# Feed-forward blocks on four PSUM banks each, the sums of their seven-product groups formed in place, and sevens in two of three feature groups of a stage's last two down blocks

## Chip, cores and metric

One core of a Trainium2 chip runs the whole program in one launch. The metric is the device time of one execution in microseconds (us); a time that is named for the kernel is the median of its runs.

## The reference

Two layers of a hybrid block on 256 rows of width 2048, all in float32: a mixer (gated delta rule and a linear recurrence in layer 0, two attentions in layer 1) and behind each mixer a feed-forward part of inner width 5632. Only the feed-forward parts and the norms beside them matter here:

```python
def swiglu(hn, w_gate, w_up, w_down):
    return (jax.nn.silu(hn @ w_gate) * (hn @ w_up)) @ w_down
...
    for layer in range(DEPTH):
...
            h = h + gdn_rglru_mixer(rmsnorm(h, ab_norm[j]), ab_w_in[j], ab_conv_qkv[j], ab_a_log[j],
...
            h = h + fox_moba_mixer(rmsnorm(h, cd_norm[j]), cd_w_in[j], cd_f_bias[j], cd_w_out[j])
        h = h + swiglu(rmsnorm(h, ffn_norm[layer]), ffn_w_gate[layer], ffn_w_up[layer], ffn_w_down[layer])
    return rmsnorm(h, final_norm)
```

## The kernel before, in words

**Split operands.** Every weight tile is loaded as float32 (128x1024: 256 rows of the contraction by 512 columns, 0.5 MB), rounded by ScalarE to `hi` (`whi` or `thi`, L547), and VectorE subtracts to get `lo` (`wlo` or `tlo`, L560). The activations are kept as such a pair too: `X` (the mixer's output, normed), `hid` (silu(gate)*up, turned). A product takes three TensorE passes, x_hi·w_hi, x_hi·w_lo and x_lo·w_hi (L419 to L421), all 128 rows by 512 columns.

**Plain steps and sevens.** A feed-forward block makes a 256x1024 result (two row halves t, two column halves i, so four PSUM banks `F[t,i]`). It is a *gate/up* block (512 gate and 512 up columns, contraction 2048 from `X`, four feature groups of 512) or a *down* block (1024 columns of the output, contraction over the `hid` of the stage, three or four feature groups). A *plain* step takes one weight tile and serves both row halves: 12 matmuls. A feature group done plainly is four such steps, 48 matmuls. A group done *by sevens* is seven steps of one product each, six matmuls a step, 42 in all: it multiplies sums of the activation quarters (`comb`, made ahead by `combine`) by sums of the weight tiles b11, b12, b22 and b21.

**Where the sevens accumulate.** Four of the seven products are needed in more than one of the four results. They go to banks `M0` to `M3` of their own (pool `msp`, four banks, tag `ms`), and the other three to `F` (pool `acc`, four banks). At the block's end `ends` copies M0 out and adds M2, M3 and M1 into a 128x4x512 tile `e` in SBUF (L431 to L434); `values` then adds each `F` to `e`, applies the scales and silu and multiplies (L721, L722, L727); `residual` adds `h` to `e` and then `F` (L741, L746). The banks of one block are freed by these reads, and the next block takes the same `acc` and `ms` banks.

**Weight sums.** In a seven VectorE forms T = b11+b12 (L485), T += b22 and T += b21 (L492); b12+b22 is made by one accumulating DMA from GpSimd's queue (L487). `load` (L166) gives each tile a buffer of `wr` (three) or `raw4` (four); it runs inside `ahead`, four steps ahead of the step's matmuls, and the first 12 loads of a phase take `wr` alone (`loads[0] = -12` in `phase`, L74).

**Order.** `ffn` (L657) runs 11 gate/up blocks and 6 down blocks as three stages of 4, 4 and 3 gate/up blocks with two down blocks behind each. `groups` and `down` say how many feature groups go by sevens: none in the first block, two of four in the others, two in the down blocks of the first two stages and one of three in those of the last. `steps` mixes plain steps and sevens, three plain steps in front and three behind. From the second block on VectorE, ScalarE and TensorE run in the order written (`stream`, `manual_schedule`); before that the scheduler places the instructions. SyncE (SP) issues all loads in one queue, and a load that waits for its buffer holds those behind it.

**Around it.** The mixer's last projection ends with `norm_then`: for each 512 columns `sumsq` squares `h` into a scratch tile `junk` (L316 to L319), and `to_x` transposes `h` into `X` (L328 to L330). A mixer phase and a feed-forward phase use the same SBUF space for their pools, so a tile of the feed-forward phase outside `wr` can be written only when the last reader or writer of what lay there is done.

Of the kernel before, what the change touches and what calls it, by code (L numbers as in the profile page):

```python
# [47 lines left out]
def body(tc, A, out):  # L48
# [266 lines left out]
    def sumsq(g, *ts):  # L315
        for t in ts or range(2):  # L316
            j = (mx.tile([128, 1024], F32, name="junk", tag="T", bufs=2)[:, 0:512] if more else
                 mx.tile([128, 512], F32, name="junk", tag="t2", bufs=4))
            S.activation(j, h[:, t, g * 512:(g + 1) * 512], AF.Square, accum_out=ssp[:, t, g:g + 1])  # L319
# [69 lines left out]
    def combine(f, r=None):  # L389

        c = mx.tile([128, 4, 2, 128], F32, name="cc4", tag="T", bufs=2)
# [12 lines left out]
    def combine_x(x4, r=None):  # L404

        f = mx.tile([128, 4, T], F32, name="cf", tag="T", bufs=2)
# [31 lines left out]
    class Step:  # L438


        def __init__(self, high, use, unit=None):
            self.high, self.use, self.unit = high, use, unit

    def steps(src, x, comb, nd, early, late):

        ns = len(comb)
        plain = [(i, u) for m in range(nd) if m not in comb for u in (2 * m, 2 * m + 1) for i in range(2)]
        n, F, M = len(plain) // 2, {}, {}

        def bank(t, i):  # L450
            if (t, i) not in F:
                F[t, i] = Bank(acc.tile([128, 512], F32, name=f"F{t}{i}", tag="acc"), n + (ns if t * i == 0 else 0))
            return F[t, i]

        def bank7(j):
            if j not in M:
                M[j] = Bank(ms([128, 512], f"M{j}"), ns)
            return M[j]

        def xs(k, t):  # L460
            return [x(k)[:, j, t * 128:(t + 1) * 128] for j in range(2)]

        def high(i, u, b, name):
            def f():
                b[name] = load(src(i, u))
                return b[name]
            return f

        def simple(i, u):
            b = {}  # L470

            def use(w, tt=(0, 1)):
                for t in tt:
                    bank(t, i).add(lambda kk: xs(2 * u + kk, t), w)
            return Step(high(i, u, b, "b"), use, (i, use))

        def seven(m):
            b = {}
            cx = lambda i: lambda kk: [comb[m]()[:, j, i, kk] for j in range(2)]
            q = lambda j, t: lambda kk: xs(4 * m + 2 * j + kk, t)  # L480

            def first():
                load_b12()
                b["t"] = mx.tile([128, 1024], F32, name="T", tag="T", bufs=2)
# [1079 lines left out]
```

## Time and profile before

| | |
|---|---|
| median of 3 runs | 2218.5 us (2218.19 to 2218.76) |
| span of the profiled execution, first to last instruction | 2217.3 us, 1.2 under the median of the runs; its own time is not listed apart |
| TensorE, VectorE, ScalarE busy | 99%, 88%, 60% |
| feed-forward part of layer 0, first to last matmul | 430.3 to about 1098 us |
| feed-forward part of layer 1 | 1517.5 to 2208.2 us |
| loads there, 0.5 MB each | 264 a part from SP, 30 accumulating ones a part from GpSimd |

A busy time is a union of what the profile records; a matmul's record is longer than the distance to the next one, so TensorE's rate is read from the starts of its instructions and not from its busy share. A row of the timeline gives start, length, engine, line and form; in brackets stands the engine's idle time before it and what ended it.

### The profile page before, as it was taken

To read this page: it belongs to the slowest core of one execution; us is meant where nothing else is said; L and a number is where in the kernel's file an instruction comes from. 1 tells how busy PE (TensorE), PEld (TensorE's weight loads), DVE (VectorE), ACT (ScalarE), POOL (GpSimd) and SP (SyncE) were. 2 spreads that over 40 slices of the span, in tenths; PEclk is the share of its full clock that TensorE was granted. 3 is DMA by queue.
4 is the path that set the end of the run, shared out by engine and by line. 5 is a ranking of instruction groups with operands and counts; after the bars stand their busy time and mean duration, and the time that the engine had idled before them with its cause. 6 is when DMAs were issued, how large, how long until landed. Compare 5 with 4: busy or idle time off the path is not lost.

```text
span 2217.3 us, 30619 instructions
## 1 busy us (share of the span) xinstructions
PE 2200.4 (99%) x10960; PEld 1840.2 (83%) x10960; DVE 1961.3 (88%) x2664; ACT 1333.7 (60%) x1787; POOL 54.0 (2%) x66
## 2 busy tenths in 40 slices
PE   9999999999999999999999999999999999999998
PEld 8888888888888888888888888888888888888886
DVE  8899676679999999999996688857899999999998
ACT  6786664556655666466664554545666566655665
POOL 0000000000000000000000000000000000000000
PEclk9999999999999999999999999999999999999999
DMA  7545446667777778677664565556678777777784
GB/s 284 158 145 167 136 151 188 204 210 222 235 226 247 211 215 246 214 229 235 195 201 154 154 188 171 162 181 218 204 214 237 232 224 222 237 224 233 232 243 138
DMA packets 126569, 453.79 MB, mean 205 GB/s; under 512 B 14128, under 2 KB 15664, under 8 KB 126288
## 3 DMA queue, kind: packets, MB, share of 16 engines
q1 hardware_dynamic: 117488, 420.10, 58.2%
q0 software_dynamic: 8640, 31.46, 8.5%
q8 instruction: 86, 1.41, 0.3%
q14 instruction: 67, 0.55, 0.1%
q10 hardware_dynamic: 288, 0.27, 0.0%
HBM read 449.68 MB, written 2.10 MB: 204 GB/s over the span
## 4 chain that ended last, share of the span: by engine, by line
PE 88%; DVE 8%; issue 2%; DMA 1%; ACT 1%; DVEq 0%; ACTq 0%; POOLq 0%; SPq 0%
PE F L420 14%; PE F L419 14%; PE F L421 14%; PE Pw L201 11%; PE Pw L206 6%; PE M L421 5%; PE M L419 5%; PE M L420 5%; PE Px L305 3%; PE Px L307 3%; PE Px L306 3%; DVE wlo L560 1%; PE Ph L673 1%; DVE e L721 1%; DVE tlo L560 1%
## 5 line engine op out<-in xcount | busy, mean ns | idle before, releaser
L181 ACT CAST whi<-raw 128x1024 fp32r<-128x1024 f32 x245 | 256.8, 1051 | 261.7 <-PE Pw L201 85.3
L547 ACT CAST whi<-raw 128x1024 fp32r<-128x1024 f32 x362 | 372.0, 1048 | 51.1 <-PE F L421 31.1
L182 DVE TENSOR_TENSOR wlo<-raw,whi 128x1024 fp32r<-128x1024 f32 x245 | 299.0, 1222 | 114.7 <-PE Pw L206 37.2
L201 PE MATMUL Pw<-X,whi 128*128 128x512 f32 x1088 | 388.3, 400 | 0.0
L206 PE MATMUL Pw<-X,wlo 128*128 128x256 f32 x1088 | 304.6, 280 | 0.2
L419 PE MATMUL F<-whi,X 128*128 128x512 f32 x698 | 273.1, 391 | 0.6 <-DVE h L746 0.6
L421 PE MATMUL F<-whi,X 128*128 128x512 f32 x698 | 272.1, 390 | 0.0
L560 DVE TENSOR_TENSOR wlo<-raw,whi 128x1024 fp32r<-128x1024 f32 x214 | 260.6, 1220 | 9.2 <-ACT whi L547 5.3
L420 PE MATMUL F<-wlo,X 128*128 128x512 f32 x650 | 253.2, 390 | 0.0
L201 PEld LDWEIGHTS Pw<-X,whi 128*128 128x128 f32 x1088 | 204.2, 188 | 47.2 <-issue 0.5
L547 ACT CAST whi<-T 128x1024 fp32r<-128x1024 f32 x110 | 116.1, 1055 | 197.2 <-DVE T L492 119.1
L206 PEld LDWEIGHTS Pw<-X,wlo 128*128 128x128 f32 x1088 | 205.3, 189 | 1.6 <-DVE wlo L182 0.7
L560 DVE TENSOR_TENSOR tlo<-raw,whi 128x1024 fp32r<-128x1024 f32 x148 | 180.6, 1220 | 7.9 <-ACT whi L547 6.0
L547 ACT CAST thi<-raw 128x1024 fp32r<-128x1024 f32 x166 | 173.5, 1047 | 13.6 <-PE F L421 8.7
L419 PEld LDWEIGHTS F<-whi,X 128*128 128x128 f32 x698 | 131.1, 188 | 27.7 <-issue 1.1
L421 PEld LDWEIGHTS F<-whi,X 128*128 128x128 f32 x698 | 131.0, 188 | 27.3
L547 ACT CAST thi<-T 128x1024 fp32r<-128x1024 f32 x70 | 74.0, 1057 | 130.9 <-DVE T L485 61.9
L492 DVE TENSOR_TENSOR T<-T,raw 128x1024 f32<-128x1024 f32 x120 | 146.7, 1223 | 1.7
L420 PE MATMUL F<-tlo,X 128*128 128x512 f32 x370 | 144.1, 389 | 0.3 <-DVE tlo L379 0.3
L420 PEld LDWEIGHTS F<-wlo,X 128*128 128x128 f32 x650 | 122.1, 188 | 24.9
L560 DVE TENSOR_TENSOR wlo<-raw,thi 128x1024 fp32r<-128x1024 f32 x102 | 124.5, 1221 | 8.5 <-PE F L420 4.4
L419 PE MATMUL F<-whi,hid 128*128 128x512 f32 x336 | 131.3, 391 | 0.0
(445 smaller groups left out, 4691.1 us busy)
## 6 DMA issues: line engine op xcount, KB each, us to landing
raw<-in_gu SPq DMA_DIRECT2D x352, 512.0 KB, 4.6
raw<-in_dn SPq DMA_DIRECT2D x176, 512.0 KB, 4.7
raw<-in_w0w SPq DMA_DIRECT2D x72, 512.0 KB, 3.7
raw<-in_wo SPq DMA_DIRECT2D x64, 512.0 KB, 3.6
raw<-in_w1w SPq DMA_DIRECT2D x64, 512.0 KB, 3.6
raw<-in_gu POOLq DMA_DIRECT2D x40, 512.0 KB, 7.8
raw<-in_w1x SPq DMA_DIRECT2D x32, 512.0 KB, 3.7
raw<-in_dn POOLq DMA_DIRECT2D x20, 512.0 KB, 7.3
```

The lines of the kernel that those rows point to most:

```text
L181: S.copy(hi, raw)
L182: V.tensor_sub(lo, raw, hi.bitcast(F32))
L201: PE.matmul(P.rearrange("p a b -> p (a b)"), hi[:, kk], X[:, k].rearrange("p a b -> p (a b)"), start=k == 0, stop=False)
L206: PE.matmul(P[:, 0], lo[:, kk], X[:, k, 0], start=False, stop=k == NK - 1)
L305: PE.matmul(Ps[t], x[:, 0, ts], hi[:, kk], start=k == 0, stop=False)
L306: PE.matmul(Ps[t], x[:, 0, ts], lo[:, kk], start=False, stop=False)
L419: PE.matmul(self.t, xh, hi[:, kk], start=self.i == kk == 0, stop=False)
L420: PE.matmul(self.t, xh, lo[:, kk], start=False, stop=False)
L421: PE.matmul(self.t, xl, hi[:, kk], start=False, stop=kk == 1 and self.i == self.n - 1)
L492: V.tensor_tensor(out=b["t"], in0=b["t"], in1=b[name], op=ALU.add)
L547: S.copy(y.hi, y.raw)
L560: V.tensor_sub(y.lo, y.raw, y.hi.bitcast(F32))
```

## The change

**Four banks a block.** A block's class is `Mix`. Its sevens use only the four `F` banks: the seven products go there in an order in which the shared ones are turned into the sums they are needed in, in PSUM itself (`middle`: one copy out of `F[0,0]`, four VectorE sums of 512 columns, one copy back into `F[0,1]`), and the other products and the plain steps are added on top. Blocks alternate between the pools `acc` and `msp`; `Ph`, the transposes of a block's result, lies in the block's own pool. `ends`, `e` and the sums with `F` behind it are gone from the feed-forward part: `values` applies silu from PSUM and multiplies from PSUM, `residual` adds `F` to `h`.

**Order.** A seven is split in two: four *early* steps (y0 to y3) and three *direct* ones (y4 to y6). The early steps of a block are interleaved with the last four plain steps of the block before it, two early steps to one plain.

**Weight sums.** T is gone: b11 becomes b11+b12 and then b11+b12+b22 in place, and b21 is added by a second accumulating DMA. Tiles b11, b12, b22 get buffers `ha`, `hb`, `hc` (two each), and `ha` is held from y0 to y6. Other tiles take `raw`: five buffers, three of them in `wr`. `loads_to` issues loads eight steps ahead.

**Sevens.** `down` of the last stage becomes (2, 2): two of three feature groups in its two down blocks, in each of the two feed-forward parts.

**Tiles.** `junk`, `cc4`, `cf` and the transposed copy use new tags `a` and `de`, `hid` is allocated once, and GpSimd's descriptor space is set to 8192 bytes.

```diff
@@ sumsq
-            j = (mx.tile([128, 1024], F32, name="junk", tag="T", bufs=2)[:, 0:512] if more else
+            j = (mx.tile([128, 1024], F32, name="junk", tag="a", bufs=1)[:, 0:512] if more else
...
+            sevens = [self.seven(m) for m in comb]
+            self.early = [y[i] for i in range(4) for y in sevens]
+            self.direct = [y[i] for i in range(4, 7) for y in sevens]
...
+            k = 2 * u + i
+            return Step(("raw", "ha", "raw", "hb", "raw", "hc")[k % 6] if first and k < 10 else "raw",
+                        lambda raw: nc.sync.dma_start(raw, self.src(i, u)), use, unit=(i, use))
...
+            def first_sum():
+                V.tensor_tensor(out=b["b11"], in0=b["b11"], in1=b["b12"], op=ALU.add)
                 G.dma_start(b["b12"], src(1, 2 * m + 1), accum_op=ALU.add)
...
+            def third_sum():
+                G.dma_start(b["b11"], src(0, 2 * m + 1), accum_op=ALU.add)
+
+            y = [Step("ha", get("b11", 0, 2 * m), lambda w: self.add(0, 0, q(0, 0), w)),
+                 Step("hb", get("b12", 1, 2 * m), lambda w: self.add(0, 1, cx(0), w), first_sum),
+                 Step("hc", get("b22", 1, 2 * m + 1), lambda w: self.add(1, 1, cx(2), w), second_sum, third_sum),
+                 Step(None, None, lambda w: self.add(1, 0, cx(1), w), lambda: b["b12"]),
+                 Step(None, None, lambda w: self.add(0, 1, cx(3), w), lambda: b["b22"]),
+                 Step("raw", get("b21", 0, 2 * m + 1), lambda w: self.add(0, 0, q(1, 0), w)),
+                 Step(None, None, lambda w: self.add(1, 0, q(1, 1), w), lambda: b["b11"])]
+            y[1].needs, y[2].needs, y[3].needs, y[6].needs = [y[0]], [y[1]], [y[1]], [y[2]]
+            y[0].free, y[1].free, y[2].free = y[6], y[3], y[4]
...
+            def sums():
+                d, e = (o["d"][:, j] for j in range(2))
+                V.tensor_tensor(out=d, in0=F[1, 1], in1=d, op=ALU.add)
+                V.tensor_tensor(out=e, in0=F[0, 1], in1=d, op=ALU.subtract)
...
+                V.tensor_tensor(out=F[1, 1], in0=e, in1=F[1, 0], op=ALU.subtract)
+                V.tensor_tensor(out=F[1, 0], in0=F[1, 0], in1=d, op=ALU.add)
...
+                    y.raw = (wr.tile([128, 1024], F32, name="raw") if y.tag == "raw" and count_raw[0] % 5 in (0, 2, 4) else
+                             mx.tile([128, 1024], F32, name=y.tag, tag=y.tag, bufs=2))
...
-        for groups, down in (((0, 2, 2, 2), (2, 2)), ((2, 2, 2, 2), (2, 2)), ((2, 2, 2), (1, 1))):
+        for groups, down in (((0, 2, 2, 2), (2, 2)), ((2, 2, 2, 2), (2, 2)), ((2, 2, 2), (2, 2))):
...
+        for Y in blocks:
+            e = list(Y.early)
+            r = -(-len(e) // len(tail)) if tail else 0
+            while e or tail:
+                order += e[:r] + tail[:1]
+                e, tail = e[r:], tail[1:]
+            cut = max(len(Y.plain) - 4 * (Y is not blocks[-1]), 0)
+            d, body, tail = list(Y.direct), Y.plain[:cut], Y.plain[cut:]
...
+            while d or body:
+                order += d[:2] + body[:1]
+                d, body = d[2:], body[1:]
```

**What moves, first place: the start of a feed-forward part.** SP's queue at the end of layer 0's mixer and the first loads of the feed-forward part. `in_wo0` is the mixer's last weight, `in_gu0` the gate/up weight; before, the first tile of the first block is raw_4622, followed by the second and third.

```order
143 L175 DMA raw_4564<-in_wo0 128x1024 [waits DMAHW0_49,DVE_49]
144 L175 DMA raw_4622<-in_gu0 128x1024 [waits DMAHW1_49,DVE_49,Activation_49]
145 L175 DMA raw_4626<-in_gu0 128x1024 [waits DMAHW2_49,DVE_49]
146 L175 DMA raw_4632<-in_gu0 128x1024 [waits DMAHW3_49,DVE_49]
147 L175 DMA raw_4638<-in_gu0 128x1024 [waits DMAHW4_49,DVE_49]
```

And now, where the tile of the first step is raw_4620, that of the second ha_4622, and raw_4624, raw_4632 and raw_4668 are those of the third, seventh and ninth:

```order
143 L175 DMA raw_4564<-in_wo0 128x1024 [waits DMAHW0_49,DVE_49]
144 L488 DMA raw_4624<-in_gu0 128x1024 [waits DMAHW1_49,DVE_49,Activation_49]
145 L488 DMA raw_4632<-in_gu0 128x1024 [waits DMAHW2_49,DVE_49]
146 L488 DMA raw_4668<-in_gu0 128x1024 [waits DMAHW3_49,DVE_49]
147 L488 DMA raw_4620<-in_gu0 128x1024 [waits PE_49,Activation_49]
148 L488 DMA ha_4622<-in_gu0 128x1024
```

The first step's tile, which went ahead of the others into `wr`, now stands fourth and lies in the feed-forward phase's own space. The wait on Activation of row 147 is for the mixer's very last `junk` (L319, second row half of the last 512 columns). The same stands at the start of layer 1's part. TensorE's queue at that place before (Px: the mixer's projection, Pt: transposes of h, F00: first bank):

```order
2063 L307 MATMUL Px1_4489<-whi_4566,Od_3334 128x512
2064 L419 MATMUL F00_4650<-whi_4624,X_77 128x512
2065 L328 MATMUL Pt_4588<-tab_78,h_76 128x128
2066 L328 MATMUL Pt_4593<-tab_78,h_76 128x128
2067 L328 MATMUL Pt_4598<-tab_78,h_76 128x128
2068 L328 MATMUL Pt_4603<-tab_78,h_76 128x128
2069 L420 MATMUL F00_4650<-wlo_4630,X_77 128x512
```

And now (whi_4636 and wlo_4640 are made of raw_4620):

```order
2071 L328 MATMUL Pt_4603<-tab_78,h_76 128x128
2072 L473 MATMUL F00_4654<-whi_4636,X_77 128x512
2073 L473 MATMUL F10_4661<-whi_4636,X_77 128x512
2074 L474 MATMUL F00_4654<-wlo_4640,X_77 128x512
2075 L475 MATMUL F00_4654<-whi_4636,X_77 128x512
```

All eight transposes now stand ahead of the first step, and every later matmul stands behind that step.

**Second place: between the last two down blocks of a part.** VectorE's queue in layer 0's part before; the second block's first sum is T_10076:

```order
1308 L560 TENSOR_TENSOR wlo_10030<-raw_10001,thi_10003 128x1024
1309 L746 TENSOR_TENSOR h_76<-F00_9814,e_10019 128x512
1310 L746 TENSOR_TENSOR h_76<-F10_9821,e_10019 128x512
1311 L560 TENSOR_TENSOR tlo_10050<-raw4_10026,whi_10028 128x1024
1312 L746 TENSOR_TENSOR h_76<-F01_9835,e_10019 128x512
1313 L746 TENSOR_TENSOR h_76<-F11_9842,e_10019 128x512
1314 L485 TENSOR_TENSOR T_10076<-raw4_10046,raw_10074 128x1024
```

And now; ha_9548 and ha_9560 are the b11 buffers at y6 of the last but one block, ha_9842 and ha_9866 the same two buffers at y0 of the last:

```order
1258 L774 SCALAR_TENSOR_TENSOR a_9815<-F01_9349,rs_4808,a_9815 128x512
1259 L774 SCALAR_TENSOR_TENSOR a_9815<-F11_9389,rs_4808,a_9815 128x512
1260 L620 TENSOR_TENSOR tlo_9834<-ha_9548,whi_9820 128x1024
1261 L620 TENSOR_TENSOR wlo_9846<-ha_9560,thi_9832 128x1024
1262 L620 TENSOR_TENSOR tlo_9876<-ha_9842,whi_9844 128x1024
1263 L748 TENSOR_TENSOR hid_4619<-Ph_9854,hid_4619 128x4x128
1264 L748 TENSOR_TENSOR hid_4619<-Ph_9859,hid_4619 128x4x128
1265 L620 TENSOR_TENSOR wlo_9890<-ha_9866,whi_9874 128x1024
1266 L503 TENSOR_TENSOR ha_9842<-ha_9842,hb_9870 128x1024
1267 L620 TENSOR_TENSOR wlo_9904<-raw_9868,thi_9888 128x1024
```

With two of three groups by sevens the last but one block has no plain step between its direct steps and the early steps of the next, so the lo parts of y6 (rows 1260 and 1261), which free the two `ha` buffers, stand right ahead of those of y0 that need the same buffers loaded anew.

More of the change, by code (lines that the diff above doesn't have):

```diff
@@ L438, in body, with __init__ @@
     class Step:
[L441 to L469, printed above, removed]
+        def __init__(self, tag, load, use, ready=None, after=None, unit=None):
+            self.tag, self.load, self.use, self.ready, self.after, self.unit = tag, load, use, ready, after, unit
+            self.needs, self.free = [], self
@@ L505, in steps @@
-        sevens = [y for m in comb for y in seven(m)]
-        plain = [simple(*y) for y in plain]
-        if not sevens:
-            return plain, F, M
-        mid = len(plain) - early - late
-        order = plain[:early]
-        for g in range(mid + 1):
-            order += sevens[g * len(sevens) // (mid + 1):(g + 1) * len(sevens) // (mid + 1)]
-            order += plain[early + g:early + g + 1] if g < mid else plain[early + mid:]
-        return order, F, M
+                    self.add(t, i, lambda kk: self.xs(2 * u + kk, t), w)
@@ L779, in ffn @@
+                space = (msp, "ms") if len(blocks) % 2 else (acc, "acc")
+                if j < piece:
+                    Y = Mix(lambda i, u, b=b: gu[b, u, i], lambda k: X[:, k], {m: lambda m=m: cx[m] for m in range(groups[j])}, 4,
+                            *space, first=b == 0)
+                    Y.after = values(Y, hid, j, j < max(down))
                     b += 1
@@ L804, in ffn @@
-                if h1:
-                    acts.append(h1)
-        stream(acts, guard)
+                    Y = Mix(lambda i, u, u0=2 * (b - piece), p=p: dn[2 * p + i, u0 + u], lambda k: hid[:, k],
+                            {m: lambda m=m: ch[m] for m in range(down[p])}, piece, *space)
+                    Y.after = residual(Y, p)
+                blocks.append(Y)
+        if fin:
+            Y.after = []
+            by_halves(Y.plain[-3:])
+        order, tail = [], []
+        for Y in blocks:
[6 more added lines that the diff above has]
+            d, body, tail = list(Y.direct), Y.plain[:cut], Y.plain[cut:]
+            Y.first = (d + body + tail)[0]
+            while d or body:
+                order += d[:2] + body[:1]
+                d, body = d[2:], body[1:]
+            events += (Y.middle() if Y.ns else []) + Y.after
@@ new lines, in ffn @@
+        where = {id(y): k for k, y in enumerate(order)}
+        puts = {}
+        put = lambda k, *f: puts.setdefault(k, []).extend(f)
+        for y, w, f in events:
+            put(where[id(y)] + 1 + w, f)
+        p0 = [where[id(y)] for y in blocks[0].plain]
+        put(p0[5], lambda: cx.update({0: combine_x(X[:, 0:4])}))
+        put(p0[8], rstd)
+        put(p0[10], lambda: cx.update({1: combine_x(X[:, 4:8])}))
+        Z, Y = blocks[-2:]
+        q = where[id(Y.first)]
+        if fin:
+            put(where[id(Z.first)] + 4, lambda: then(None))
+            for i in range(4):
+                put(q - 5 + i, lambda i=i: then(i, True))
+            put(q + 3, lambda: then(0))
+            put(q + 5, lambda: then(1))
+        else:
+            put(q + 2, lambda: then(0), lambda: then(1))
@@ L808, in ffn @@
+        stream(order, puts, blocks[1].early[0])
         if not fin:
```

278 lines of the change are left out of this document (137 added, 141 removed).

## The prediction

> **What bounds the kernel now.** The page first:
>
> ```profile
> span 2217.3 us, 30619 instructions
> PE 2200.4 (99%) x10960; PEld 1840.2 (83%) x10960; DVE 1961.3 (88%) x2664; ACT 1333.7 (60%) x1787; POOL 54.0 (2%) x66
> ```
>
> Then the busy time by stage (columns: stretch, its length, busy us and instructions of TensorE, its weight loads, VectorE, ScalarE and GpSimd, granted clock, DMA share, GB/s), here for 600 us inside layer 0's feed-forward part:
>
> ```profile
> 475.00:1075.00 600.00, 598.04 (x2679) 494.51 (x2678) 581.51 (x566) 366.89 (x408) 24.17 (x28) 1.00 0.76 227
> ```
>
> TensorE lacks 2 us of 600 and VectorE only 18.5. Whether TensorE's 99% is its full rate is read from the starts in its timeline; this is the first feed-forward step behind layer 0's mixer:
>
> ```profile
> 430.29 0.39 PE L419 MATMUL F<-whi,X 128*128 128x512 f32 x1
> 430.56 0.66 PE L328 MATMUL Pt<-tab,h 128*128 128x128 f32 x4
> 430.97 0.48 PE L420 MATMUL F<-wlo,X 128*128 128x512 f32 x1
> 431.65 0.48 PE L421 MATMUL F<-whi,X 128*128 128x512 f32 x1
> 431.97 0.40 PE L419 MATMUL F<-whi,X 128*128 128x512 f32 x1
> 432.20 0.39 PE L420 MATMUL F<-wlo,X 128*128 128x512 f32 x1
> 432.43 0.39 PE L421 MATMUL F<-whi,X 128*128 128x512 f32 x1
> 432.66 0.39 PE L419 MATMUL F<-whi,X 128*128 128x512 f32 x1
> 432.88 0.39 PE L420 MATMUL F<-wlo,X 128*128 128x512 f32 x1
> ```
>
> From 431.97 to 432.88 four matmuls start, 0.227 us apart; that is the price of a 128x512 matmul. The part is bound by TensorE's count of matmuls, and what it loses beside them is in the waits that ended on TensorE (layer 0's part, then layer 1's; columns: total, times, longest):
>
> ```profile
> PE Ph L673 <- DVE e L727: 1.4, 4, 0.5
> PE F L419 <- DVE h L746: 0.6, 1, 0.6
> ...
> PE Ph L673 <- DVE e L727: 1.3, 4, 0.4
> ```
>
> **The change, part by part.** The sum is made against the profiled execution, whose span of 2217.3 lies 1.2 us under the runs' median of 2218.5; that difference is kept.
>
> *Fewer matmuls.* GpSimd's accumulating loads, one for each group by sevens, count the groups now:
>
> ```profile
> L487 POOL DMA_DIRECT2D raw<-in_gu x40: 862/862/1005, 467.7 to 2122.1; - x40
> L487 POOL DMA_DIRECT2D raw<-in_dn x20: 862/862/867, 604.2 to 2180.5; - x20
> ```
>
> 60 groups become 64 (two down blocks in each of two parts, one group more in each). A group saves 48 - 42 = 6 matmuls: 24 x 0.227 = **-5.4 us**, all on the engine that bounds.
>
> *Waits removed.* The transposes Ph wait because ends, the four adds, two activations and a product stand in a row before them; now silu and product read PSUM and the transposes come four steps later. The wait of F on L746 was for a bank; blocks now alternate between pools. All nine go: 1.4 + 0.6 + 1.3 = 3.3 us of idle, and as idle counts from the end of a record (0.39) and not from the next possible start (0.227), 9 x 0.16 = 1.4 more: **-4.7 us**. Bounds: if the transposes still wait as long, only the 0.8 of the bank goes; more than 4.7 isn't there to win.
>
> *VectorE.* Of the three sums of a group one goes to a DMA, and the tile-wide adds of block ends go too:
>
> ```profile
> L492 DVE TENSOR_TENSOR T<-T,raw 128x1024 f32<-128x1024 f32 x120 | 146.7, 1223 | 1.7
> L560 DVE TENSOR_TENSOR wlo<-raw,whi 128x1024 fp32r<-128x1024 f32 x97 | 118.1, 1220 | 1.8 <-ACT whi L547 1.7
> L685 DVE TENSOR_TENSOR hid<-Ph,hid 128x512 fp32r<-128x512 f32 x22 | 14.1, 686 | 2.1 <-ACT e L681 2.0
> ```
>
> 60 x 3 - 64 x 2 = 52 sums of 1.22 us fall away, 12 lo parts of 1.22 come (seven splits for four, four times), so VectorE's work falls by 49 us over both parts even before the block ends. I cost this at nothing: VectorE had room for TensorE's rate already.
>
> *The start of each part.* Here a wait is added. Before, the first tile lay in `wr` and was split before the mixer ended, so TensorE went from the mixer's last matmul to the first step. Now that tile is loaded behind the mixer's last `junk`, and everything on TensorE stands behind it. When `junk` ends is seen on VectorE, which waits for it today, in both layers:
>
> ```profile
> 431.97 1.23 DVE L407 TENSOR_TENSOR cf<-X 128x1024 f32<-128x1024 f32 x1 [0.79 <-ACT junk L319]
> ```
>
> ```profile
> 1519.24 1.23 DVE L407 TENSOR_TENSOR cf<-X 128x1024 f32<-128x1024 f32 x1 [0.79 <-ACT junk L319]
> ```
>
> The time from issue to landing is that of the loads just before, which find the queues empty (416 to 430 us); the second row is the burst behind (428 to 445 us):
>
> ```profile
> DMA to landing us min/median/max: 3.5/3.5/3.6
> ```
>
> ```profile
> DMA to landing us min/median/max: 3.6/5.6/6.7
> ```
>
> Then come the split's two halves, 1.22 on VectorE (above) and on ScalarE:
>
> ```profile
> L547 ACT CAST whi<-raw 128x1024 fp32r<-128x1024 f32 x165 | 169.4, 1048 | 16.3 <-PE F L421 12.3 <-DMA raw<-in_dn 2.3 <-DMA raw<-in_gu 0.5
> ```
>
> So issue 431.97, landed 435.5, hi at 436.5, lo at 437.8. On hi alone two matmuls can run; the third needs lo. At 437.8 TensorE has done 2; before, it had done 3 by 431.97 and 3 + 5.83/0.227 = 28.7 by 437.8. It is 26.7 x 0.227 = 6.1 us behind, and since it runs at its full rate afterwards nothing is won back. Behind the waiting load stand all later loads of SP's queue; late next is the second tile, issued right behind, with the first step's 2.7 us of matmuls to cover it. Two parts: **+12.2 us**. Bounds: 3.4 us in place of 3.5 at best (+11.9 in all); the burst's 5.6 at worst (+16.4).
>
> *The last two down blocks.* Each has two groups by sevens and four plain steps, which all lie between early steps. So six direct steps of six matmuls (1.36 us each) and eight transposes are followed at once by y0 of the next block:
>
> ```profile
> 480.47 0.87 PE Ph L673 x8
> ```
>
> y0's tile needs the buffer that y6's lo part reads. I take time 0 at the end of the last plain step and VectorE's rows 1258 to 1267 in order: the product, two times 0.69 (as L685 above, also from PSUM) to 1.4; lo of the two y6 at 2.6 and 3.8; y0's load issued at 2.6 lands at 6.2, hi 7.2, lo 8.5; TensorE reaches y0 at 6 x 1.36 + 0.87 = 9.0: no wait. Next the two turned parts (1.4) to 9.9, lo of the second y0 at 11.1, which TensorE wants at 9.0 + 1.36 + 0.23 = 10.6: 0.5 wait. Next a sum (12.3) and lo of the plain step at 13.6, wanted at 12.4: 1.2 wait. Together 1.7 a part, **+3.4 us**. Bounds: 0, if VectorE runs earlier than here; 4 a part, if the load takes the burst's 5.6. At other block ends four plain steps (10.9 us) stand between y6 and y0 and cover all of this.
>
> *More traffic.* b21 is read twice: 34 accumulating loads more in each part (64 - 30). Their price:
>
> ```profile
> q1 hardware_dynamic: 117488, 420.10, 58.2%
> q0 software_dynamic: 8640, 31.46, 8.5%
> ```
>
> 8.5% of 2217 us over 60 is 3.1 us of all 16 engines for one, against 1.6 for a plain one (58.2% over 420.10/0.524 = 801). 34 x 3.1 = 107 us on some 680 raise the DMA share from 0.76 to about 0.92. The landing of an accumulating load is
>
> ```profile
> DMA to landing us min/median/max: 5.8/7.5/10.8
> ```
>
> and from y1's sum to y3 stand six steps (10.9 us), and operands are made four steps ahead (some 7 us more); from y2 to y6 some twelve. I take 0, as the loads are issued eight steps ahead; the upper bound is a rival below. The copies of `middle` go to ScalarE, idle 40%; GpSimd's issues, 0.86 us each, double in a queue that holds nothing else there. Both at nothing.
>
> Sum: -5.4 - 4.7 + 12.2 + 3.4 = **+5.5**, span 2222.8, runs **2224.0 us**.
>
> [...] At the end of the program the clock is seen to fall (the last matmul ends at 2208.2):
>
> ```profile
> 2208.20:2209.90 1.70, 0.00 (x0) 0.00 (x0) 1.63 (x6) 1.63 (x5) 0.00 (x0) 1.00 0.01 5
> 2209.90:2211.50 1.60, 0.00 (x0) 0.00 (x0) 1.39 (x7) 1.08 (x5) 0.00 (x0) 1.00 0.78 289
> 2211.50:2213.20 1.70, 0.00 (x0) 0.00 (x0) 1.36 (x2) 1.28 (x2) 0.00 (x0) 0.50 1.02 376
> ```
>
> After 3.3 idle us it is halved. At a part's start TensorE will idle from 431.9 to 436.5, 4.6 us. And at the program's start, where it worked from 2.7 us on, 128x256 matmuls start 0.23 apart up to about 6.5 us and 0.12 apart after:
>
> ```profile
> 2.70:4.50 1.80, 1.77 (x4) 1.17 (x4) 0.11 (x1) 0.00 (x0) 0.00 (x0) 1.00 0.96 357
> ```
>
> ```profile
> 6.15 0.43 PE L248 MATMUL Pw<-X,whi 128*128 128x256 f32 x1
> 6.38 0.34 PE L249 MATMUL Pw<-X,wlo 128*128 128x256 f32 x1
> 6.55 0.28 PE L248 MATMUL Pw<-X,whi 128*128 128x256 f32 x1
> 6.67 0.28 PE L249 MATMUL Pw<-X,wlo 128*128 128x256 f32 x1
> ```
>
> So about 3.8 us pass before it is whole again. That makes the first rival: at half speed for 3.8 us, 1.2 of them waiting for lo anyway, a part loses 1.3 more: 2.6 in all, 2226.6 us. For it speaks 4.6 > 3.3; against it that one end shows one distance, and the clock may look at fixed stretches that an idle time has to fill. [...]
>
> **Other rivals.** *Not slower:* between the last two down blocks VectorE is early enough, the wait is 0 and the sum +2.1: 2220.6 us, within what can be told. It decides at 1.1 us a part. For it: VectorE's slack everywhere else; against it: its queue there, written out above. *DMA decides:* at a share of 0.92 loads land later; if accumulating loads take over some 18 us, ScalarE waits at y3 with all casts behind it, in 32 blocks with sevens; 0.5 us each gives +16, 2240 us. Against it: 357 GB/s were moved in the row of 2.7 to 4.5 us above, and about 253 are needed here (227 + 34 x 0.524 MB in 680 us). *The start costs nothing*, the load finding its space free earlier: -6.7, 2211.8 us; against it stands the wait in SP's queue.
>
> **How the numbers follow.** Forecast 0.42, clock rival 0.15, DMA rival 0.05: slower 0.62. The not slower rival 0.29. No cost at the start, 0.09. About 0.2% (4.4 us) is what a measurement of this kernel tells from no change. Low end: 11.9 for the starts, nothing between the down blocks, and 2 us of doubt on that: 2218.5 - 10.1 + 11.9 - 2 = 2218. High end: -10.1 + 16.4 + 2.6 + 4.6 (2.3 a part between the blocks) = +13.5, 2232. Outside lie the last two rivals, some 0.14.
>
> **What would show it.** Right: TensorE idle for 4 to 5 us behind the mixers, released by a load's cast; idle of 1 to 2 us between the last down blocks; no wait of Ph on VectorE; 24 matmuls fewer. Wrong: TensorE without that idle, or waits on accumulating loads all over the part.

## The result and the profile after

| | before | after |
|---|---|---|
| median of the runs | 2218.63 us (4 runs, 2218.19 to 2219.56) | 2236.48 us (4 runs, 2235.58 to 2238.61) |
| ratio, 95% interval | | 1.0082 (1.0068 to 1.0096) |
| span of the profiled execution | 2217.3 us | 2236.8 us |

The changed kernel is 17.9 us slower; the forecast was 5.5. First the page, with the two lines that answer to those shown of before:

```profile
span 2236.8 us, 30625 instructions
PE 2205.6 (99%) x10936; PEld 1841.2 (82%) x10936; DVE 1852.5 (83%) x2584; ACT 1353.7 (61%) x1793; POOL 113.1 (5%) x134
```

TensorE has 24 instructions fewer (10936 for 10960) and VectorE 109 us less to do. Both are as the text said, and yet the span is 19.5 us longer. What TensorE waited for, layer 0's part first, then layer 1's (total, times, longest):

```profile
PE F L473 <- ACT whi L608: 5.1, 1, 5.1
PE F L474 <- DVE wlo L620: 1.3, 2, 0.7
PE F L474 <- DVE tlo L620: 0.8, 1, 0.8
```

```profile
PE F L473 <- ACT whi L608: 8.1, 2, 5.6
PE F L474 <- DVE tlo L620: 1.5, 2, 0.8
PE F L474 <- DVE wlo L620: 0.3, 1, 0.3
```

The waits of `Ph` and of a bank are gone. In their place stand one wait of 5.1 and one of 5.6 us for a cast at the two starts, one of 2.5 us for a cast at layer 1's border between the last two down blocks, and short ones for lo parts. These are 17.1 us together. The rest doesn't show as a wait. It shows in the number of `F` matmuls in the 25 us from the last matmul of the mixer's projection on (columns as in the stages above, the number in brackets behind TensorE's busy time), before and after, layer 0 and layer 1:

```profile
430.06:455.06 25.00, 24.27 (x105) 19.70 (x106) 0.00 (x0) 0.00 (x0) 1.00 0.79 268
1517.33:1542.33 25.00, 24.29 (x105) 19.70 (x106) 0.00 (x0) 0.00 (x0) 1.00 0.80 272
```

```profile
431.78:456.78 25.00, 18.03 (x65) 14.19 (x66) 0.00 (x0) 0.00 (x0) 0.86 0.77 288
1525.30:1550.30 25.00, 17.55 (x67) 13.85 (x68) 0.00 (x0) 0.00 (x0) 0.86 0.77 292
```

40 and 38 matmuls are missing: at 0.227 us, 9.1 and 8.6, that is 17.7 us for the two starts. The last column but two is the granted clock, 0.86 where it was 1.00. Layer 0's start cut into stretches, all engines:

```profile
433.90:438.40 4.50, 0.00 (x0) 0.00 (x0) 4.18 (x11) 2.05 (x5) 0.00 (x0) 1.00 0.81 262
438.40:441.80 3.40, 3.05 (x6) 1.99 (x7) 3.10 (x3) 3.40 (x5) 0.00 (x0) 0.50 1.02 411
441.80:445.25 3.45, 3.45 (x9) 2.64 (x8) 3.45 (x4) 3.15 (x4) 0.00 (x0) 0.50 1.03 412
445.25:448.65 3.40, 3.40 (x16) 2.82 (x15) 2.56 (x3) 1.36 (x2) 0.00 (x0) 1.00 1.03 412
```

TensorE has nothing to do for 4.5 us, and then, with work at hand, starts 9 matmuls in 3.45 us where it starts 16 when the clock is whole. The busy time doesn't tell (3.45 of 3.45); the number does.

The border is measured in the same way, over 20 us from the transposes `Ph` of the last gate/up block on, in layer 0 and 1:

```profile
1080.72:1100.72 20.00, 17.22 (x70) 12.62 (x70) 0.00 (x0) 0.57 (x1) 1.00 0.56 156
2173.93:2193.93 20.00, 15.87 (x59) 11.65 (x59) 0.00 (x0) 0.58 (x1) 0.91 0.59 187
```

A kernel without a wait there (the one with tiles of their own for y0, below) does 86 in the same 20 us. 16 and 27 are missing, 3.6 and 6.1 us; in layer 1 the clock of 0.91 is a part of it. Why y0 is late there is read from its two loads and the row of the cast that waits for the first (start, length, engine, line and form, in brackets the idle time before it and its end):

```profile
L499 SPq DMA_DIRECT2D ha<-in_dn x2: 328/328/328, 2172.2 to 2173.4; - x2
...
DMA to landing us min/median/max: 8.2/8.2/8.3
```

```profile
2180.53 1.04 ACT L608 CAST whi<-ha 128x1024 fp32r<-128x1024 f32 x1 [9.38 <-DMA ha<-in_dn]
...
2181.62 0.50 PE L473 MATMUL F<-whi,hid 128*128 128x512 f32 x1 [2.56 <-ACT whi L608]
```

In layer 0 the same two loads:

```profile
DMA to landing us min/median/max: 5.7/5.7/5.8
```

The prediction let this load land 3.6 us behind its issue, as into empty queues. It took 8.2 here, and 5.7 in layer 0. The rest of its row held: counted from the end of the last plain step (1076.63 and 2169.85), the load was issued at 2.4 us (2.6 worked out), and TensorE came to y0 at 9.1 in both layers (9.0 worked out). Only the landing moved, from 6.2 to 8.0 and 10.6.

### The profile page after: what moved, and what is told of

Read it like the earlier page. It is cut to its first block, busy times and chain, and to the rows that moved or that the text cites. A ratio compares the mean times of both kernels' runs of the same rounds, so it can differ in the third digit from the quotient of the medians.

```text
span 2236.8 us, 30625 instructions
## 1 busy us (share of the span) xinstructions
PE 2205.6 (99%) x10936; PEld 1841.2 (82%) x10936; DVE 1852.5 (83%) x2584; ACT 1353.7 (61%) x1793; POOL 113.1 (5%) x134
## 3 DMA queue, kind: packets, MB, share of 16 engines
q1 hardware_dynamic: 117488, 420.10, 54.0%
q0 software_dynamic: 18432, 67.12, 17.3%
## 4 chain that ended last, share of the span: by engine, by line
PE 93%; DVE 3%; DMA 1%; ACT 1%; issue 1%; DVEq 0%; ACTq 0%; SPq 0%
PE F L474 20%; PE F L473 20%; PE F L475 20%; PE Pw L201 10%; PE Pw L206 5%; PE Px L305 3%; PE Px L307 3%; PE Px L306 3%; PE F L420 1%; PE F L421 1%; PE F L419 1%; PE Ph L735 1%; DVE wlo L182 1%; PE Psc L1365 1%; DMA raw<-in_w0w 0%
## 5 line engine op out<-in xcount | busy, mean ns | idle before, releaser
L181 ACT CAST whi<-raw 128x1024 fp32r<-128x1024 f32 x245 | 256.6, 1050 | 262.4 <-PE Pw L201 78.9
L182 DVE TENSOR_TENSOR wlo<-raw,whi 128x1024 fp32r<-128x1024 f32 x245 | 298.6, 1220 | 115.5 <-PE Px L306 38.0
L608 ACT CAST whi<-ha 128x1024 fp32r<-128x1024 f32 x174 | 183.6, 1056 | 202.1 <-DVE ha L503 54.2
L473 PE MATMUL F<-whi,X 128*128 128x512 f32 x688 | 270.3, 393 | 10.7 <-ACT whi L608 10.7
L608 ACT CAST whi<-raw 128x1024 fp32r<-128x1024 f32 x212 | 221.8, 1054 | 92.9 <-PE F L475 74.1
L474 PE MATMUL F<-wlo,X 128*128 128x512 f32 x588 | 230.8, 392 | 0.1
L474 PE MATMUL F<-tlo,X 128*128 128x512 f32 x420 | 163.6, 390 | 0.0
L620 DVE TENSOR_TENSOR wlo<-raw,whi 128x1024 fp32r<-128x1024 f32 x128 | 155.6, 1218 | 5.0 <-ACT whi L608 1.7
L620 DVE TENSOR_TENSOR wlo<-ha,whi 128x1024 fp32r<-128x1024 f32 x104 | 127.0, 1222 | 33.4 <-ACT whi L608 24.1
L608 ACT CAST thi<-raw 128x1024 fp32r<-128x1024 f32 x114 | 119.9, 1052 | 35.5 <-PE F L475 28.7
L473 PE MATMUL F<-whi,comb 128*128 128x512 f32 x352 | 136.9, 389 | 0.0
L475 PE MATMUL F<-whi,comb 128*128 128x512 f32 x352 | 136.9, 389 | 0.0
L608 ACT CAST thi<-ha 128x1024 fp32r<-128x1024 f32 x86 | 91.0, 1058 | 72.6 <-DVE ha L503 26.4
L473 PE MATMUL F<-thi,X 128*128 128x512 f32 x320 | 125.3, 391 | 0.0
```

The source lines that it names most:

```text
L181: S.copy(hi, raw)
L182: V.tensor_sub(lo, raw, hi.bitcast(F32))
L473: PE.matmul(P, xh, hi[:, kk], start=z[0] == 1 and kk == 0, stop=False, skip_group_check=skip)
L474: PE.matmul(P, xh, lo[:, kk], start=False, stop=False, skip_group_check=skip)
L475: PE.matmul(P, xl, hi[:, kk], start=False, stop=kk == 1 and z[0] in z[1:], skip_group_check=skip)
L608: S.copy(y.hi, y.raw)
```

## The experiments

The theory after the result: (1) the start of a part costs what was worked out, 6 us of waiting, and 2 to 3 more by the halved clock; (2) the border waits longer than worked out because y0's load, issued late, also stands behind other transfers; (3) the savings and the zeros are right. The rivals: traffic that costs all over the part, a clock that falls for another reason, and a border that is VectorE's row of work alone. All ratios are against runs of the kernel before on the same chip, whose medians lie between 2218.6 and 2219.3 us; differences between two runs of this text are of medians, if nothing else is said.

### First tiles in wr

```diff
-            return Step(("raw", "ha", "raw", "hb", "raw", "hc")[k % 6] if first and k < 10 else "raw",
+            return Step(("raw", "raw", "raw", "ha", "hb", "hc", "raw", "raw", "ha", "hb")[k] if first and k < 10 else "raw",
...
-                    y.raw = (wr.tile([128, 1024], F32, name="raw") if y.tag == "raw" and count_raw[0] % 5 in (0, 2, 4) else
+                    y.raw = (wr.tile([128, 1024], F32, name="raw") if y.tag == "raw" and count_raw[0] % 5 in (1, 2, 3) else
```

> The changed kernel, but the first tiles of a feed-forward part lie in wr again, so that they are loaded before the mixer ends. Theory (the start of a part costs about 8.4 us: 5.2 to 5.6 of idle, 0.8 of waiting for lo, the rest at half clock): TensorE goes without a gap over 1 us from the mixer into the part, the clock stays at 1.00 there, and the time falls by 17 to about 2219.5 us (2217 to 2222). Rival, the traffic (the loss lies in loads that land late all over the part): under 3 us less, 2233 or more. Rival, the clock falls there for another reason than the idle: the idle goes, the halves stay, about 2225.

Measured: 2220.22 us, ratio 1.0004 (0.9995 to 1.0012), 16.3 less than the changed kernel. The 25 us from the mixer's last projection matmul on are as before the change, and so is the clock:

```profile
429.98:454.98 25.00, 24.28 (x104) 19.41 (x105) 0.00 (x0) 0.00 (x0) 1.00 0.81 294
1514.84:1539.84 25.00, 24.28 (x105) 19.70 (x106) 0.00 (x0) 0.00 (x0) 1.00 0.84 310
```

The edit puts the first three tiles of a part into `wr`. So the loss at the start hangs on where the first tiles lie, and the halved clock goes with the wait. The traffic is unchanged in this kernel, so it isn't the traffic.

### The kernel before with a late first tile

```diff
-        loads[0], extra[0] = -12, 0
+        loads[0], extra[0] = -12 if mixer else 0, 0
```

> The kernel before, but the first tile of each feed-forward part lies in raw4, in space that the mixer's last scratch tile used, so its load waits as in the changed kernel. Theory (8.4 us a part, the clock included): 2218.6 + 17 = about 2235.5 us, with a gap of 5 to 6 us and a halved clock for one or two stretches of 3.4 us at each start. The prediction's own size (6.1 a part, full clock): 2231. Rival (the start is dear only with the changed kernel's order of loads): under 2224.

Measured: 2234.7 us, ratio 1.0073 (1.006 to 1.0085), 15.7 more than the kernel before. Its profile, 25 us from the last projection matmul on:

```profile
431.66:456.66 25.00, 18.38 (x72) 14.89 (x73) 0.00 (x0) 0.00 (x0) 0.86 0.78 274
1526.38:1551.38 25.00, 18.36 (x69) 14.82 (x70) 0.00 (x0) 0.00 (x0) 0.86 0.78 271
```

33 and 36 matmuls are missing, and the clock is 0.86 again. The edit lets the first twelve loads of a part, the first tile's among them, take buffers of `raw4` too. In the kernel before, this makes nearly the whole of the start's loss without anything else of the change.

### The wait without the idle time

Two runs put 40 transposes of `h`, whose result isn't used, behind the mixer's own ones. In the first they wrote to a bank of `ms`:

```diff
+        D = ms([128, 4, 128], "Dm")
+        for j in range(40):
+            PE.transpose(D[:, j % 4], h[:, j % 2, 1920:2048], tb["ident"])
         stream(order, puts, blocks[1].early[0])
```

> The changed kernel with 40 transposes of 128x128 more at the end of each mixer (about 4.4 us of TensorE's time, their result is not used), which lie in the wait for the first tile. The idle time of the start is filled and nothing else is changed. Theory (a part's start costs 5.5 us of waiting and about 2.7 us more by a clock that is halved because TensorE was idle): the waiting stays, the clock stays at 1.00 at both starts, 2236.5 - 5.4 = about 2231 us. Rival (the half clock there has another cause, or its loss is hidden in the waits for lo): 2235 to 2238.

Measured: 2235.95 us, ratio 1.0078 (1.0065 to 1.0091). It doesn't separate the theory from its rival: that bank was still held by the mixer, so the transposes began 1.8 us late, took 6.1 us in layer 0 (where the clock was halved for 3.4 us under them) and 4.6 in layer 1, and held up the part's first matmul. In layer 0 that came at 441.51, 9.5 us behind the mixer's last one and not 6.9 as in the changed kernel. The second run takes a bank that nothing holds:

```diff
-        D = ms([128, 4, 128], "Dm")
+        D = acc.tile([128, 4, 128], F32, name="Dm", tag="acc")
```

> The run with a busy start once more, with its 40 extra transposes in a bank that no copy of the mixer holds, so that they begin at once and end before the first tile is split (at full clock 40 take 4.4 us of a wait of 4.9 to 5.6). Theory (the idle time halves the clock, and that costs 2.5 us a part on top of the wait): no halved stretch at either start, first matmuls of the part where the changed kernel has them, 2236.5 - 5 = about 2231.5 us (2230 to 2233.5). Rival (the start's loss is all waiting, the half clock costs nothing more): 2235 to 2238.

Measured: 2233.75 us, ratio 1.0066 (1.0053 to 1.0079): 2.7 us less than the changed kernel by the medians, 3.5 by the ratios; the expected range missed by a quarter of a us, on the theory's side of the rival. What the profile shows is plainer (the same 25 us; the transposes aren't counted):

```profile
430.87:455.87 25.00, 17.58 (x76) 14.23 (x77) 0.00 (x0) 0.00 (x0) 1.00 0.78 287
1520.94:1545.94 25.00, 17.91 (x78) 14.53 (x79) 0.00 (x0) 0.00 (x0) 1.00 0.79 291
```

The clock stays at 1.00 at both starts, and 11 more matmuls are done. In layer 0 the first matmul comes 6.9 us behind the mixer's last, as in the changed kernel, so the 11 are the clock's: 2.5 us, and 29 matmuls (6.6 us) are lost by waiting. In layer 1 the first matmul comes after 6.6 us, where the changed kernel had 7.4. These 0.9 us are 4 of the 11 matmuls, so the clock took some 7 there (1.6 us), and the waiting 31 (7.0 us). Together that is 4.1 us by the clock. By the interval of the ratios the run's time is not told apart from that of the changed kernel; in its profile a part of the gain is lost again, as layer 1's border is at half clock for 6.8 us, where the changed kernel had 3.4.

### One of three groups by sevens in the last down blocks

```diff
-        for groups, down in (((0, 2, 2, 2), (2, 2)), ((2, 2, 2, 2), (2, 2)), ((2, 2, 2), (2, 2))):
+        for groups, down in (((0, 2, 2, 2), (2, 2)), ((2, 2, 2, 2), (2, 2)), ((2, 2, 2), (1, 1))):
```

> The changed kernel with one feature group of three by sevens in a stage's last two down blocks, as before the change. 24 matmuls come back (+5.4 us). Theory (the waits at the border of the last two down blocks, 3.5 us in layer 0 and 6.2 in layer 1 with its clock drop, and 1.9 within layer 1's last block, are the doing of two groups there, because no plain step stands between y6 and the next y0): they go, 2236.5 + 5.4 - 11.6 = about 2230 us. The prediction's own size for the border, 1.7 a part: 2236.5 + 5.4 - 3.4 = 2238.5. Rival (the border waits for whatever the queues hold, sevens or not): 2242.

Measured: 2230.5 us, ratio 1.0054 (1.0041 to 1.0066), 6.0 less although 24 matmuls (5.4 us) came back. TensorE's waits of this kernel in layer 1's part are one:

```profile
PE F L473 <- ACT whi L608: 5.0, 1, 5.0
```

That is the start. The border's waits and those in the last block came with the second group.

### The third sum on VectorE

```diff
             def third_sum():
-                G.dma_start(b["b11"], src(0, 2 * m + 1), accum_op=ALU.add)
+                V.tensor_tensor(out=b["b11"], in0=b["b11"], in1=b["b21"], op=ALU.add)
+                return b["b11"]
...
-                 Step(None, None, lambda w: self.add(1, 0, q(1, 1), w), lambda: b["b11"])]
+                 Step(None, None, lambda w: self.add(1, 0, q(1, 1), w), third_sum)]
...
```

> The changed kernel with the third sum of a seven made by VectorE out of the tile of y5, as before the change: 64 accumulating loads of 0.5 MB fewer, 64 sums of 1.22 us more on VectorE (about 1930 us busy). Theory (the border of the last two down blocks is longer than 1.7 us since y0's loads stand behind a backlog to which two accumulating loads gave 3.7 us each): these loads land within 5 us of issue in place of 8.2 in layer 1, the border waits shrink to about 2 us a part, 2231 to 2234 us in all. Rival, VectorE's queue sets the border (the prediction's picture): two more sums ahead of y6's lo, the same or up to 5 us more, 2236 to 2241. Rival, the traffic costs all over the part: 2225 or less.

Measured: 2238.9 us, ratio 1.0092 (1.0077 to 1.0108), in the range of the rival, and by the intervals not told apart from the changed kernel. But the landing that the theory forecast did come: 4.7 us for 8.2, so the accumulating loads gave 3.5 us of it in all, and not 3.7 each. These are y0's loads at layer 1's border:

```profile
L499 SPq DMA_DIRECT2D ha<-in_dn x2: 327/327/327, 2172.0 to 2173.2; - x2
...
DMA to landing us min/median/max: 4.5/4.7/4.8
```

TensorE's waits in this kernel, layer 1's part:

```profile
PE F L473 <- ACT whi L609: 6.1, 2, 5.0
PE F L474 <- DVE tlo L621: 3.1, 2, 2.3
PE F L474 <- DVE wlo L621: 1.6, 3, 0.7
```

The wait for y0's cast falls from 2.5 to 1.1 us (6.1 - 5.0), and a new one of 2.3 us for a lo part appears in the last block, where VectorE now has two sums more beside the last norm's products and stands without a gap from 2202.6 to 2216 us. Both causes hold: the backlog delays the load, and VectorE's row there is full.

### A longer backlog

The load of the last norm's weight (1 MB) stands ahead of y0's loads in layer 1 alone. Built on the kernel with the first tiles in `wr`, this run makes it twice:

```diff
+            nc.sync.dma_start(fo[0][:, 0], A["fw"].to_broadcast([128, D]))
             nc.sync.dma_start(fo[0][:, 2], A["fw"].to_broadcast([128, D]))
```

> The kernel with the first tiles in wr (2220.2 us), and the load of the last norm's weight (1 MB, which stands in SP's queue ahead of y0's loads at layer 1's border) is made twice, the second time into space that is written over later. Theory (layer 1's border is longer than layer 0's because y0's tiles land behind this load; a transfer of 1 MB holds the queues for 2.5 us): layer 1's border is 2.5 us longer, and up to 1.7 more by the clock: 2222.5 to 2224.5. Rival (the border's length is VectorE's row of work): 2220 to 2221.

Measured: 2220.34 us, ratio 1.0004 (0.9996 to 1.0013), no change. The run missed its aim: in SP's queue the second load stood behind y0's two (issued at 2156.24, those at 2154.72 and 2155.86), so it says only that a transfer behind them costs nothing. The next is one load of double width:

```diff
-            nc.sync.dma_start(fo[0][:, 2], A["fw"].to_broadcast([128, D]))
+            nc.sync.dma_start(fo[0][:, 1:3], A["fw"].unsqueeze(1).to_broadcast([128, 2, D]))
```

> The run with the last norm's weight loaded twice, mended: there the second load was put behind y0's loads in SP's queue; now it is one load of double width (2 MB in place of 1) at the old place, ahead of them. Theory (the wait for y0 at layer 1's border is the queues' backlog, of which 1 MB is 2.5 us): y0's tiles land 2.5 us later, about 10.8 us behind issue, the border is 2.5 longer and the clock takes up to 1.7 more: 2220.2 + 2.5 to 4.2 = 2222.5 to 2224.5. Rival (the border's length is VectorE's row of work): 2220 to 2221.

Measured: 2222.22 us, ratio 1.0015 (1.0006 to 1.0024): 2.0 us more by the medians, 2.4 by the ratios, just under the theory's range and above the rival's. All 11 runs lie above all 11 of the kernel with a load of 1 MB (2220.98 at least, 2220.91 at most). In its profile y0's loads land later by what the extra 1 MB takes, and TensorE waits as much longer (5.29 us for the cast, where the same kernel with a load of 1 MB has 2.63):

```profile
DMA to landing us min/median/max: 10.9/11.0/11.0
```

```profile
2165.27 0.80 PE L473 MATMUL F<-whi,hid 128*128 128x512 f32 x1 [5.29 <-ACT whi L608]
```

The landing is 2.7 us later (10.9 for 8.3) and the wait 2.7 us longer. So the backlog sets layer 1's border, us for us.

### Tiles of their own for y0

The last stage uses three quarters of `hid`. The fourth holds the two y0 tiles of the last block; the first tiles are in `wr`.

```diff
-        hid = ogp.tile([128, 16, 2, T], F32R, name="hid", tag="hid")
+        hid = [ogp.tile([128, 4, 2, T], F32R, name=f"hid{j}", tag=f"hid{j}", bufs=1) for j in range(4)]
...
+                o.append(ogp.tile([128, 2, 1024], F32, name="own", tag="hid3", bufs=1))
...
+        for j, y in enumerate(blocks[-1].early[:2]):
+            y.own = lambda j=j: own(j)
```

> The kernel with the first tiles in wr, and besides the two y0 tiles of a part's last block have a place of their own (the quarter of hid that the last stage doesn't use), so that their loads need not wait for y6; two of three groups stay by sevens. Theory (the border waits since y0's load is issued only when y6 has let go of ha): no wait over 0.5 us at the borders and no halved clock there, 2220.2 less 3.3 less 6 = about 2211 us (2209 to 2213), 7 under the kernel before. Rival (the backlog in the queues sets the border whenever the load is issued): 2217 or more. Rival (VectorE's row of work there is the bound even with the tiles in place): 2214 to 2217, with waits for lo of 2 us a part.

Measured: 2209.54 us, ratio 0.9959 (0.9947 to 0.9972), 9.1 us faster than the kernel before and the fastest of all here, with the same products and the same traffic as the changed kernel. Its page and its only wait in layer 1's part:

```profile
span 2207.8 us, 30621 instructions
PE 2194.4 (99%) x10936; PEld 1837.6 (83%) x10936; DVE 1851.6 (84%) x2584; ACT 1355.6 (61%) x1793; POOL 113.1 (5%) x134
```

```profile
PE F L474 <- DVE wlo L623: 0.3, 1, 0.3
```

The same 20 us over the border, for which the changed kernel had 70 and 59:

```profile
1070.84:1090.84 20.00, 19.37 (x86) 15.95 (x86) 0.00 (x0) 0.58 (x1) 1.00 0.66 144
2152.22:2172.22 20.00, 19.37 (x86) 15.92 (x86) 0.00 (x0) 0.57 (x1) 1.00 0.82 209
```

The loads now go out over 100 us ahead (at 942.8 and 2024.1 the first ones). VectorE's row of work, which the prediction wrote out, didn't change, and makes no wait at the border once the tiles are there: even its waits for lo were waits for late tiles.

### Fewer sevens at the border, first tiles in wr

Two runs with the first tiles in `wr`, the second with (1, 1) in place of (1, 2):

```diff
-        for groups, down in (((0, 2, 2, 2), (2, 2)), ((2, 2, 2, 2), (2, 2)), ((2, 2, 2), (2, 2))):
+        for groups, down in (((0, 2, 2, 2), (2, 2)), ((2, 2, 2, 2), (2, 2)), ((2, 2, 2), (1, 2))):
```

> The kernel with the first tiles in wr, with one of three groups by sevens in the last but one down block and two of three in the last. 12 matmuls come back (+2.7 us). Theory (the border waits when nothing plain stands between y6 and y0): eight plain steps are there in the last but one block, the border is without a wait, the 1.6 us within layer 1's last block stay: 2220.2 + 2.7 - 9.5 = about 2213.5 us. Rival (two groups in the last block alone make the border wait): 2220 or more.

Measured: 2211.3 us, ratio 0.9967 (0.9954 to 0.9979). TensorE has no wait left in layer 1's part, not even the 1.6 us that were expected to stay. With plain steps between y6 and the next y0 two groups in the last block cost nothing.

> The kernel with the first tiles in wr and one of three groups by sevens in both last down blocks: as many matmuls as the kernel before, no wait at a start and none at the border. What is left of the change is the four banks a block and the sums in place. Theory (nine waits of 4.7 us in all are gone and nothing else is gained or lost): 2218.6 - 4.7 = about 2214 us (2213 to 2215). Rival (the added traffic and the casts cost somewhere what the waits gave): 2217 to 2219.

Measured: 2214.55 us, ratio 0.9982 (0.9973 to 0.9991), 4.1 us under the kernel before at an equal number of matmuls: 2.0 to 6.0 by the interval, 4.7 expected.

### The fastest with the third sum on VectorE

The kernel with tiles of its own for y0, with `third_sum` as above:

```diff
-                G.dma_start(b["b11"], src(0, 2 * m + 1), accum_op=ALU.add)
+                V.tensor_tensor(out=b["b11"], in0=b["b11"], in1=b["b21"], op=ALU.add)
+                return b["b11"]
```

> The fastest kernel so far (first tiles in wr, the last block's y0 tiles in a place of their own, 2209.5 us) with the third sum of a seven on VectorE: 64 accumulating loads fewer, 64 sums of 1.22 us more. Theory (outside the border the traffic costs nothing, and VectorE has room): 2208.5 to 2212 us. Rival (the accumulating loads cost a little all over the part, as the prediction's rival had it): under 2207. Rival (VectorE is near its bound): 2214 or more.

Measured: 2214.34 us, ratio 0.9978 (0.9969 to 0.9987), 4.8 more than with the accumulating load (4.2 by the ratios). Its waits in layer 1's part are two short ones and the one in the last block:

```profile
PE F L474 <- DVE tlo L624: 2.4, 1, 2.4
PE F L474 <- DVE wlo L624: 0.6, 2, 0.3
```

64 accumulating loads fewer gained nothing that shows: there was no other wait left to shorten. The second load of b21 is the cheaper place for that sum, as VectorE has no room for it in the last block.

## Why the prediction was wrong

Slower was right, and so was the place of both losses; the sum was off by 12 us because two of its terms were too small. The terms against what the runs gave:

| term | predicted | measured |
|---|---|---|
| fewer matmuls | -5.4 | -5.0 (2209.54 against 2214.55) |
| nine waits removed | -4.7 | -4.1 (2214.55 against the kernel before, 2.0 to 6.0) |
| start of each part | +12.2 | +16.3 (2236.48 against 2220.22) |
| last two down blocks | +3.4 | +10.7 (2220.22 against 2209.54) |
| VectorE, traffic, copies | 0 | 0, but for the backlog at the border |
| sum | +5.5 | +17.9 |

The measured column is one chain of medians from the kernel before to the changed one, so its sum is no test of its own. The profile, counted in matmuls, is one: -5.4 and -4.7, +17.7 for the starts, 9.7 for the borders and some 2 in layer 1's last block make +19.3, and the spans differ by 19.5.

**Start.** The mechanism was right, and its price as a wait nearly: 6.1 us a part worked out, 6.6 and 7.0 measured with the clock kept whole. (The first tile landed 3.8 and 4.3 us behind its issue, not 3.5.) The mis-sized term is the clock, which the forecast put at nothing and its rival at 1.3 a part. It measured 2.5 and 1.6. Two steps failed. First, whether it falls at all: the idle time is 4.8 to 5.6 us, and in the four kernels with a late first tile and nothing to fill the wait (the changed one, the kernel before with a late tile, the third sum on VectorE, one and one by sevens without `wr`) all eight starts show a halved clock. Second, how long: the rival took 3.8 us at half speed, of which 1.2 were waiting. In seven of the eight the halved stretch is 6.8 us long, in one 3.4. In the first 3.4 us of it TensorE still waits for hi and lo now and then, and the clock stays halved for 3.4 more of full work (9 matmuls in the stretch 441.80 to 445.25 above, 16 in the next).

**Border.** The price at a time 0 that suits the other rows was right only for a load into empty queues. "y0's load issued at 2.6 lands at 6.2" is the step that failed: it landed 5.7 us behind issue in layer 0, and 8.2 in layer 1. The bound taken for the worst case, the burst's 5.6, came out in layer 0 (bound 4, measured 3.6). What stood ahead of it when it was issued were the loads of hc and raw, four in each layer, which landed 1.3 us apart, and in layer 1 the 1 MB of the last norm besides. They were late because of two accumulating loads, issued some 15 us ahead of y0's: these had landed 5 us before it was issued, but the plain loads issued behind them took 7 to 9 us to land, and without them (the third sum on VectorE) 4 to 5. Behind the wait of 2.5 us that came of it in layer 1 the clock was halved once more, for 3.4 us. The zero for traffic was right for the time, and wrong as a reason: no wait outside the border, but y0's load, issued late, paid for what was queued ahead of it (8.2 us to landing in layer 1 for 4.7 without the accumulating loads). The prediction's own rival on DMA (waits at y3 in all blocks) didn't happen.

**Last block.** Some 2 us in layer 1 that no step named (the last 120 matmuls take 29.1 us, before the change 27.0). The last norm's products and the lo parts share VectorE there, and the late border adds to it: with tiles of their own for y0 0.9 us of it are left, and with one group by sevens in the block before and two in the last nothing. Which of VectorE's pieces makes the rest wasn't tried apart.

**Savings.** Both right within the runs' uncertainty, and the removed waits are absent from the profile. The "not slower" rival was wrong for the same reason as the forecast; that a start costs nothing was refuted by the 5.1 and 5.6 us in the waits.

## What to carry to other kernels

A load that has to wait for its buffer is priced by its place in the queue, not by its length: here one of 0.5 MB landed 3.8 us behind its issue at layer 0's start, and 5.7 and 8.2 at the borders, behind four loads and behind four and the 1 MB of the last norm. So count the transfers still open when it is issued. A wait of TensorE is priced by its idle time and by what the clock takes afterwards, which was 2.5 us on 6.6 and 1.6 on 7.0 here, so buffers at the joints of a program, where nothing plain stands in between, deserve space first. When a change with sound parts is slower, undo its joints and keep the parts: two edits to where a few tiles lie turned 17.9 us slower into 9.1 us faster.

## What the runs showed of the hardware

**The clock fell behind a stretch that wasn't idle throughout.** The run with the third sum on VectorE has its clock halved in the last block, in layer 1 (stretches cut where the granted clock changed, 3.41 us each):

```profile
2208.15:2211.57 3.42, 3.27 (x15) 2.38 (x13) 3.42 (x5) 2.35 (x5) 0.00 (x0) 1.00 0.00 0
2211.57:2214.98 3.41, 1.24 (x5) 1.05 (x6) 3.38 (x4) 2.38 (x4) 0.00 (x0) 1.00 0.00 0
2214.98:2218.40 3.42, 3.42 (x9) 2.59 (x8) 2.54 (x5) 3.36 (x7) 0.00 (x0) 0.50 0.00 0
```

In the stretch ahead TensorE was busy for 1.24 of 3.41 us, and the clock still fell. At the end of the run with a load of 2 MB it was busy for 1.53 of such a stretch and the clock stayed whole through the next, to fall only behind an empty one:

```profile
2210.17:2213.59 3.42, 1.53 (x7) 0.94 (x5) 2.40 (x7) 2.37 (x8) 0.00 (x0) 1.00 0.20 77
2213.59:2217.00 3.41, 0.00 (x0) 0.00 (x0) 2.27 (x7) 1.93 (x3) 0.00 (x0) 1.00 0.84 312
2217.00:2220.41 3.41, 0.00 (x0) 0.00 (x0) 0.00 (x0) 0.00 (x0) 0.00 (x0) 0.50 0.61 226
```

In the busy start's first run, layer 0, TensorE stood idle for only 1.8 us between the mixer's transposes and the added ones, and these went at half clock for a part of their 6.1 us (4.4 in the second run). These are single cases; how busy TensorE has to be for the clock to stay whole is not shown by them. All halved stretches between the starts and the end of the last block are 3.41 or 6.83 us long. The prediction held against its clock rival that the clock may look at fixed stretches which an idle time has to fill. Stretches of fixed length are seen; that an idle time has to fill one doesn't agree with the 1.24 us of work. At the starts, in seven of the eight a stretch of 3.41 us without any matmul lay ahead of the halved one; in the kernel before with a late tile, layer 0, TensorE was busy for 0.80 us of it.

**The halved stretches lie on a raster, and the cost varies.** In the changed kernel they begin at 438.41, 1530.67 and 2182.62 us: 320 and 511 times 3.413 us behind the first. By the starts of the matmuls, the clock at the program's start becomes whole between 6.5 and 10.8 us in the profiles of these kernels, each time within 0.12 us of the raster of that profile's own halved stretches. So the raster lies differently from profile to profile (6.5 us in that of the kernel before, 8.4 in the changed kernel's). Layer 1's border had one halved stretch (3.41 us) in the run with the first tiles in `wr` and two (6.83) in the one with a second load behind y0's, though the waits were 2.6 and 2.4 us. That this is due to where the raster lay is the author's estimate; no run shows it apart.

**Accumulating loads hold the queues longer.** By the page's two lines on queues, of the changed kernel:

```profile
q1 hardware_dynamic: 117488, 420.10, 54.0%
q0 software_dynamic: 18432, 67.12, 17.3%
```

67.12 MB take 17.3% and 420.10 MB 54.0%: twice as long for a byte, so one load of 0.524 MB takes 3.0 us of all 16 engines (17.3% of 2236.8 over 128) against 1.5. That agrees with the prediction's 3.1 and 1.6; what it left out is the landing of the loads behind two of them, 7 to 9 us at the border for 4 to 5 without them.
